# Two-layer SSD and dilated-attention trunk on one core: another load order and more warm-up matmuls at the start, another PSUM tile for the first group's scores, regrouped centring matmuls at the end

## The chip, the cores and the metric

The kernel runs on one core of a Trainium2 chip. The metric is the device time of one execution in microseconds, as the median of several runs. Engines are named as in the profile: PE is TensorE's matmuls, PEld its weight loads, DVE VectorE, ACT ScalarE, POOL GpSimd, SP the engine that issues most transfers (SPq is its queue).

## The reference

A batch of one, 256 tokens of width 2048, two layers. Layer 0 is a Mamba-2 SSD mixer with 64 heads in 8 groups; layer 1 is dilated sliding-window attention with keys and values made once from layer 0's output. Both layers are scaled, shifted and gated from a conditioning row `c` (adaLN), and end in a layer norm.

```python
def reference(x, c, ada_w, ada_b, ln_g, ln_b, a_in_w, a_conv_w, ..., kv_w, b_in_w, b_out_w):
    for layer in range(DEPTH):                      # 2
        shift, scale, gate = _adaln(c, ada_w[layer], ada_b[layer])   # split(silu(c) @ w + b, 3)
        h = x * (1.0 + scale) + shift
        if layer < N_A_LAYERS:
            y = _ssd_mixer(h, ...)     # proj, causal conv + silu, chunked scan, silu gate, RMS norm, out_w
        else:
            y = _dilated_mixer(h, k_sh, v_sh, b_in_w[i], b_out_w[i])
        x = _layer_norm(DEEPNORM_ALPHA * x + (1.0 + gate) * y, ln_g[layer], ln_b[layer])
        if layer == N_A_LAYERS - 1:
            k_sh, v_sh = _shared_kv(x, kv_w)
    return x
# in the scan, one chunk of 256 tokens:
cb = jnp.einsum("blgn,bsgn->blsg", cc, bc)          # the scores of a group
y_diag = jnp.einsum("blsgk,bsgkp->blgkp", cb[..., None] * decay, xc)
```

## The kernel before, in words

All weights stream from HBM in pieces of 128 x 1024 float32 (512 KB, tile `raw`, six buffers). A piece is split into a high part (`whi`, ACT, L100) and a low part (`wlo`, DVE, L102), four buffers each, and each product is the sum of high by high, high by low and low by high (L151 to L153, L190 and L193, L232 to L234). The activations (`actT`) are split in the same way. A program written in Python issues the instructions; a scheduler then sets the order on each engine from the dependences and a cost model, and `issue_after` pins an instruction behind another. Each engine works through its own order strictly in sequence. Transfers use eight completion semaphores in turn, so each issue on SP waits for the transfer eight places before it.

**Start.** Layer 0's scale and shift are not matmuls: the conditioning row is broadcast to 128 partitions by 16 matmuls against identity columns (L473, into `cps`), ACT applies SiLU (L476, `cb_`), and DVE takes 32 products of 128 x 2048 with a summed output (`araw`, L501, L503, L317), one per 128 columns of scale or shift, each from a transfer of 1 MB. Their order is scale 0, shift 0, scale 1, shift 1 and so on. Then DVE adds the bias (L322, `mod`), and ACT makes `htmp` (L522) and its high part (L524). `warm(n, at)` issues n matmuls of ones (L460) so that PE is not idle before the real work: a group ahead of the broadcast and one behind it. The first three weight pieces come in halves: `begin_piece(i)` loads the first half (L557), `end_piece(i)` the second (L560). `plain` multiplies the first halves, unsplit, with `htmp` (L572); then the first products with split weights start at L151.

**SSD stage.** For each group, `stage1` computes the scores of B and C in three blocks (L742, L743) into a PSUM tile, evicts them to `cb` (L745 with the causal mask, L746), builds the decays `seg` on ACT from `cumT` (L756, L758), multiplies them with `cb` (L759), and transposes x (L767). `stage2` multiplies `seg` and `xd` (L800, `py`). PSUM there is `mm` (four `acc` tiles) and two pools of two tiles, `aux` and `aux2`; `aux2` holds only `py`. Ahead of group 0, DVE computes softplus and the cumulative decays (L709 to L721), PE sums them (L723, L724), and SP writes them out (L734) and reads them back broadcast (`cbc`, L751). All of this is interleaved with the projection products of the next groups.

**End.** The last layer norm, for the second half of the rows, is made on PE as a sum of two matmuls per chunk of 512 columns: `plus` adds the weighted chunk by an identity (L1318), `centre` subtracts mean times weight by a diagonal (L1322); chunk 3 is done on DVE (`between`, L1326). `root` computes the reciprocal standard deviation; DVE scales the chunks (L1341) and SP stores each (L1269).

Of the kernel before, what the change touches and what calls it, by code (L numbers as in the profile page):

```python
# [9 lines left out]
F32 = mybir.dt.float32  # L10
F32R = mybir.dt.float32r
I32 = mybir.dt.int32
AF = mybir.ActivationFunctionType
ALU = mybir.AluOpType
# [4 lines left out]
P = 128  # L19
# [30 lines left out]
def trunk(ctx, tc, xT, x, c, par, cst, bias, lnrow, ada, wdt, win, wxs, wout, wk, wv, wbin, wbout, out):  # L50
# [9 lines left out]
    aux = None  # L60
# [295 lines left out]
    with ExitStack() as cA:  # L356
# [15 lines left out]
        with ExitStack() as cS:  # L372
# [78 lines left out]
            with ExitStack() as c0:  # L451
# [11 lines left out]
                at = mm.tile([P, 2, L], F32, name="acc")  # L463
                last = warm(6, at)
                crow2 = pe.tile([48, P + KT], F32R, name="crow", bufs=1)
                V.tensor_copy(crow2, crow)
                V.tensor_tensor(crow2[32:, :P], crow[32:, :P], crow2[32:, :P].bitcast(F32), op=ALU.subtract)
                with tc.tile_pool(name="ec", bufs=4, space=PSUM) as ec:
                    for n in range(4):
# [6 lines left out]
                        S.activation(cb_[:, 512 * n:512 * n + 512], cps, AF.Silu)  # L476
                    last = warm(14, at, last)
                ex = c0.enter_context(tc.tile_pool(name="ex", bufs=4, space=PSUM))
# [110 lines left out]
                fetch_x(0)  # L589
                fetch()  # L590
                fetch()
                begin_piece(0)
                begin_piece(1)
# [142 lines left out]
            def stage1(g):  # L736

                pcb = aux.tile([P, 512], F32, name="aux")[:, :384].rearrange("p (a n) -> p a n", a=3)  # L740
                bm, cm_ = bc[g][:, 0, :], bc[g][:, 1, :]
# [528 lines left out]

    diag = pc2.tile([P, 512], F32, name="sc0", bufs=1)[:, :P]
    eps, sd = sm.tile([P, 1], F32, name="nm"), sm.tile([P, 1], F32, name="den")
# [51 lines left out]
    def between(mv):  # L1324
        V.tensor_scalar(diag, ident, mv[:, 0:1], -1.0, op0=ALU.mult, op1=ALU.mult)
        return V.scalar_tensor_tensor(u[1][:, chunk[3]], u[1][:, chunk[3]], mv[:, 0:1], lnt[:, 0, chunk[3]],  # L1326
                                      op0=ALU.subtract, op1=ALU.mult)

    plus(1, plus(0, end))
    _, r1, step = root(1, between)  # L1330
    centre(0)
    plus(2, centre(1))
    for h in range(2):
        centre(2, slice(256 * h, 256 * h + 256))
    for c in chunk:
        scaled(0, c)
        nc.gpsimd.dma_start(rows(out, 0)[:, c], u[0][:, c], accum_op=ALU.add)
    for n, h0, h1 in ((0, 0, 512), (1, 0, 512), (3, 0, 512), (2, 0, 256), (2, 256, 512)):
        c = slice(512 * n + h0, 512 * n + h1)
        with tc.issue_after(step.ins):  # L1340
            step = V.scalar_tensor_tensor(u[1][:, c], cen[n][:, h0:h1] if n < 3 else u[1][:, c], r1, lnt[:, 1, c],  # L1341
                                          op0=ALU.mult, op1=ALU.add)
        store(1, c)
# [95 lines left out]
```

## Time and profile before

| | |
|---|---|
| median of 3 runs | 1226.51 us (1226.43 to 1226.7) |
| profiled execution | 1226.18 us, span 1224.4 us |
| PE, PEld, DVE, ACT busy | 99%, 85%, 83%, 58% of the span |
| transfers | 331.45 MB read, 3.23 MB written, mean 273 GB/s over the span |
| chain that ended last | PE 83%, DMA 9%, DVE 5%, ACT 2% |

A row of the timeline gives start, duration, engine, line, operation, tiles and count; in brackets stands how long the engine had been idle and what ended that. A float32 matmul leaves two records of PE. Ends of matmuls are modelled, so successive ones overlap. In the table of stretches the columns are the stretch, its length, PE's busy time with the count of matmuls, the granted clock, the busy share of the transfer engines and GB/s; where no engine is chosen, PE, PEld, DVE, ACT and POOL stand in this order ahead of the clock. A row of waits gives the sum, the number and the longest wait.

### The profile page before, as it was taken

What the parts mean: (1) busy time and instruction counts of PE and PEld (TensorE: products, weight loads), DVE (VectorE), ACT (ScalarE), POOL (GpSimd) and SP (SyncE); (2) the same over time, 40 slices, a digit from 0 to 9 for tenths busy, and PEclk for the clock granted to TensorE, in tenths of its full rate; (3) what the DMA queues carried; (4) which work ended last, traced back from release to release, by engine and by line L of the source; (5) the groups of instructions that cost most, each with busy time, mean ns of one, the idle gap of its engine ahead of it and who ended that gap; (6) DMA issues with size and microseconds to landing.
All of it is one profiled execution on the core that took longest, in us unless ns stands there. A gap on an engine that the chain in (4) does not pass through costs nothing.

```text
span 1224.4 us, 19063 instructions
## 1 busy us (share of the span) xinstructions
PE 1210.7 (99%) x7244; PEld 1039.0 (85%) x7244; DVE 1018.5 (83%) x1448; ACT 707.2 (58%) x1058; POOL 3.9 (0%) x8
## 2 busy tenths in 40 slices
PE   8899999999999999999999999999999999999998
PEld 7889988898888888878888888888888888888886
DVE  6999996999988989899778588888987875756886
ACT  4555477878597789754445455444435844444751
POOL 0000000000000000000000000000000000000001
PEclk9999999999999999999999999999999999999999
DMA  9999986687666556689998669989997885365673
GB/s 370 422 421 422 421 279 246 228 300 246 222 205 206 172 173 208 214 322 328 390 308 295 222 194 345 344 343 385 369 389 279 285 262 174 111 193 161 194 258 69
DMA packets 81372, 335.94 MB, mean 274 GB/s; under 512 B 9200, under 2 KB 9984, under 8 KB 68480
## 3 DMA queue, kind: packets, MB, share of 16 engines
q1 hardware_dynamic: 80496, 333.59, 75.3%
q0 software_dynamic: 576, 1.05, 0.6%
q8 instruction: 57, 0.93, 0.3%
q14 instruction: 35, 0.29, 0.1%
q10 hardware_dynamic: 208, 0.08, 0.0%
HBM read 331.45 MB, written 3.23 MB: 273 GB/s over the span
## 4 chain that ended last, share of the span: by engine, by line
PE 83%; DMA 9%; DVE 5%; ACT 2%; issue 1%; SPq 0%; ACTq 0%; DVEq 0%
PE acc L190 24%; PE acc L224 24%; PE acc L193 12%; DMA raw<-in_win 5%; PE acc L233 4%; PE acc L234 4%; PE acc L232 4%; DMA araw<-in_ada 3%; DVE araw L317 2%; DVE wlo L102 1%; PE acc L153 1%; PE acc L151 1%; PE py L800 1%; PE acc L152 1%; ACT whi L100 1%
## 5 line engine op out<-in xcount | busy, mean ns | idle before, releaser
L100 ACT ACTIVATE whi<-raw 128x1024 fp32r<-128x1024 f32 x389 | 408.9, 1057 | 355.0 <-PE acc L190 106.5
L102 DVE TENSOR_TENSOR wlo<-raw,whi 128x1024 fp32r<-128x1024 f32 x389 | 469.3, 1220 | 136.2 <-ACT whi L100 126.0
L190 PE MATMUL acc<-actT,whi 128*128 128x512 f32 x1280 | 401.1, 394 | 0.0
L193 PEld LDWEIGHTS acc<-actT,wlo 128*128 128x128 f32 x1280 | 239.5, 188 | 52.5 <-DVE wlo L102 0.3
L193 PE MATMUL acc<-actT,wlo 128*128 128x256 f32 x1280 | 254.7, 280 | 0.0
L317 DVE SCALAR_TENSOR_TENSOR araw<-araw,cb__72 128x2048 f32<-128x2048 f32 x95 | 216.9, 2284 | 2.7 <-DMA araw<-in_ada 2.3
L190 PEld LDWEIGHTS acc<-actT,whi 128*128 128x128 f32 x1280 | 194.7, 188 | 0.8
L224 PE MATMUL acc<-whi,actT 128*128 128x512 f32 x560 | 144.4, 392 | 0.5 <-ACT whi L100 0.5
L224 PEld LDWEIGHTS acc<-whi,actT 128*128 128x128 f32 x560 | 104.1, 188 | 22.1 <-ACT whi L100 0.9
L233 PE MATMUL acc<-wlo,actT 128*128 128x512 f32 x272 | 107.0, 393 | 2.6 <-DVE wlo L102 2.6
L151 PE MATMUL acc<-actT,whi 128*128 128x256 f32 x372 | 103.2, 281 | 1.2 <-ACT s L657 1.0
L232 PE MATMUL acc<-whi,actT 128*128 128x512 f32 x272 | 104.3, 394 | 0.0
L224 PE MATMUL acc<-wlo,actT 128*128 128x512 f32 x384 | 103.5, 391 | 0.0
L153 PE MATMUL acc<-actT,wlo 128*128 128x256 f32 x372 | 101.7, 282 | 1.6 <-DVE wlo L102 1.4
L152 PE MATMUL acc<-actT,whi 128*128 128x256 f32 x372 | 102.8, 279 | 0.0
L234 PE MATMUL acc<-whi,actT 128*128 128x512 f32 x256 | 100.2, 391 | 0.0
L224 PEld LDWEIGHTS acc<-wlo,actT 128*128 128x128 f32 x384 | 71.6, 188 | 14.5
L151 PEld LDWEIGHTS acc<-actT,whi 128*128 128x128 f32 x372 | 69.6, 188 | 2.7 <-ACT s L657 1.4
L153 PEld LDWEIGHTS acc<-actT,wlo 128*128 128x128 f32 x372 | 68.8, 188 | 2.9 <-DVE wlo L102 2.7
L152 PEld LDWEIGHTS acc<-actT,whi 128*128 128x128 f32 x372 | 70.5, 189 | 0.5 <-issue 0.2
L233 PEld LDWEIGHTS acc<-wlo,actT 128*128 128x128 f32 x272 | 51.1, 188 | 14.7 <-DVE wlo L102 4.5
L232 PEld LDWEIGHTS acc<-whi,actT 128*128 128x128 f32 x272 | 50.7, 188 | 9.9
(321 smaller groups left out, 1296.3 us busy)
## 6 DMA issues: line engine op xcount, KB each, us to landing
araw<-in_ada SPq DMA_DIRECT2D x96, 1024.0 KB, 7.4
raw<-in_win SPq DMA_DIRECT2D x109, 512.0 KB, 6.2
raw<-in_wout SPq DMA_DIRECT2D x64, 512.0 KB, 5.8
raw<-in_wbin SPq DMA_DIRECT2D x64, 512.0 KB, 4.2
raw<-in_wxs SPq DMA_DIRECT2D x48, 512.0 KB, 4.5
raw<-in_wv SPq DMA_DIRECT2D x48, 512.0 KB, 6.8
raw<-in_wk SPq DMA_DIRECT2D x48, 512.0 KB, 8.1
cbc<-cumd SPq DMA_DIRECT2D x16, 512.0 KB, 5.6
```

What stands on the lines that cost most here:

```text
L100: copied.append(S.activation(hi, raw, AF.Copy))
L102: latest.append(V.tensor_tensor(lo, raw, hi.bitcast(F32), op=ALU.subtract))
L151: T.matmul(o, hi[:, k, c_], ahi[:, kt, :], start=first, stop=False, skip_group_check=True)
L152: T.matmul(o, hi[:, k, c_], alo[:, kt, :], start=False, stop=False, skip_group_check=True)
L153: T.matmul(o, lo[:, k, c_], ahi[:, kt, :], start=False, stop=kt == k1 - 1, skip_group_check=True)
L190: T.matmul(ps[n], hi[:, k, n * P:n * P + P], both(kt), start=kt == 0, stop=False, skip_group_check=True)
L193: T.matmul(ps[n][:, 0, :], lo[:, k, n * P:n * P + P], high(kt), start=False, stop=kt == KT - 1, skip_group_check=True)
L224: T.matmul(ps[b], a_(kt)[:, b * P:b * P + P], w_[:, k, :], start=a_ is ahi and w_ is hi and kt == k0, stop=w_ is lo and kt == k1 - 1)
L232: T.matmul(o, h_, hi[:, k, :], start=kt == k0, stop=False, skip_group_check=part)
L233: T.matmul(o, h_, lo[:, k, :], start=False, stop=False, skip_group_check=part)
L234: end = T.matmul(o, l_, hi[:, k, :], start=False, stop=kt == k1 - 1, skip_group_check=part)
L317: return V.scalar_tensor_tensor(raw, raw, 1.0, cb_, op0=ALU.mult, op1=ALU.mult, accum_out=mod[layer][:, ct, j:j + 1])
```

## The change

Four edits.

1. Seven more warm-up matmuls: 11 instead of 6 ahead of the broadcast, 16 instead of 14 behind it.
2. The first half of weight piece 0 is loaded ahead of the second adaLN scale.
3. The scores of SSD group 0 go to a tile of `aux2` (named `py`) instead of one of `aux`.
4. At the end all three `plus` products precede the `centre` products; the diagonal is made by ACT from a negated identity (`minus`, made earlier by DVE) instead of by DVE; chunk 3 is scaled first.

```diff
                 at = mm.tile([P, 2, L], F32, name="acc")
-                last = warm(6, at)
+                last = warm(11, at)
...
-                    last = warm(14, at, last)
+                    last = warm(16, at, last)
...
                 fetch()
                 fetch_x(0)
                 fetch()
+                begin_piece(0)
                 fetch()
-                begin_piece(0)
                 begin_piece(1)
...
-                pcb = aux.tile([P, 512], F32, name="aux")[:, :384].rearrange("p (a n) -> p a n", a=3)
+                pcb = aux2.tile([P, 512], F32, name="py") if g == 0 else aux.tile([P, 512], F32, name="aux")
+                pcb = pcb[:, :384].rearrange("p (a n) -> p a n", a=3)
...
-    diag = pc2.tile([P, 512], F32, name="sc0", bufs=1)[:, :P]
+    pair = pc2.tile([P, 512], F32, name="sc0", bufs=1)
+    diag, minus = pair[:, :P], pair[:, P:2 * P]
+    V.tensor_scalar(minus, ident, -1.0, None, op0=ALU.mult)
...
     def between(mv):
-        V.tensor_scalar(diag, ident, mv[:, 0:1], -1.0, op0=ALU.mult, op1=ALU.mult)
+        S.activation(diag, minus, AF.Copy, scale=mv[:, 0:1])
...
-    plus(1, plus(0, end))
+    plus(2, plus(1, plus(0, end)))
     _, r1, step = root(1, between)
     centre(0)
-    plus(2, centre(1))
+    centre(1)
...
-    for n, h0, h1 in ((0, 0, 512), (1, 0, 512), (3, 0, 512), (2, 0, 256), (2, 256, 512)):
+    for n, h0, h1 in ((3, 0, 512), (0, 0, 512), (1, 0, 512), (2, 0, 256), (2, 256, 512)):
```

Lines behind the third edit move down by one, those behind the fourth by three: L742 becomes L743, L800 becomes L801, L1341 becomes L1344.

What this does to the order is seen at three places. First SP's transfers at the start, before (`araw` are adaLN pieces, `raw` weight pieces, here halves; DMAHW0 to 7 are the eight semaphores):

```order
L310 DMA araw_180<-in_ada 128x2048
L490 DMA xt_182<-in_xT 128x512
L310 DMA araw_184<-in_ada 128x2048
L310 DMA araw_186<-in_ada 128x2048
L557 DMA raw_188<-in_win 128x512
L557 DMA raw_190<-in_win 128x512
L310 DMA araw_192<-in_ada 128x2048 [waits DMAHW0_49]
```

and after:

```order
L310 DMA araw_187<-in_ada 128x2048
L490 DMA xt_189<-in_xT 128x512
L310 DMA araw_191<-in_ada 128x2048
L557 DMA raw_193<-in_win 128x512
L310 DMA araw_195<-in_ada 128x2048
L557 DMA raw_197<-in_win 128x512
L310 DMA araw_199<-in_ada 128x2048 [waits DMAHW0_49]
```

The first half piece and the second scale have changed places; the rest of the queue stands as it was.

Second, PE in the last product of z for group 0 (`acc`, with the high and low weights `whi` and `wlo`), before:

```order
L232 MATMUL acc_1965<-whi_1987,actT_84 128x512 [waits Activation_49]
L232 MATMUL acc_1966<-whi_1987,actT_84 128x512
L233 MATMUL acc_1965<-wlo_1988,actT_84 128x512 [waits DVE_49]
L234 MATMUL acc_1965<-whi_1987,actT_84 128x512
L233 MATMUL acc_1966<-wlo_1988,actT_84 128x512
```

and after (`bcm` are B and C of group 0):

```order
L232 MATMUL acc_1972<-whi_1994,actT_84 128x512 [waits Activation_49]
L232 MATMUL acc_1973<-whi_1994,actT_84 128x512
L743 MATMUL py_2283<-bcm_1878 128x2x128 [waits DVE_49]
L744 MATMUL py_2283<-bcm_1878 128x128
L233 MATMUL acc_1972<-wlo_1995,actT_84 128x512 [waits DVE_49]
L234 MATMUL acc_1972<-whi_1994,actT_84 128x512
```

The scores stand about 195 matmuls earlier than before, in front of a product that waits for DVE. On DVE the end of the decay chain (`araw` is its scratch, `dtT` and `cumT` its results) reads before:

```order
L717 SCALAR_TENSOR_TENSOR araw<-araw 128x128 [waits DVE_49]
L718 SCALAR_TENSOR_TENSOR araw<-araw 128x128 [waits DVE_49]
L719 SCALAR_TENSOR_TENSOR dtT<-vv,araw 128x128 [waits DVE_49]
L721 SCALAR_TENSOR_TENSOR araw<-dtT,araw 128x128 [waits DVE_49]
L102 TENSOR_TENSOR wlo<-raw,whi 128x1024 [waits DMAHW0_49,Activation_49]
```

and after:

```order
L717 SCALAR_TENSOR_TENSOR araw<-araw 128x128 [waits DVE_49]
L746 TENSOR_TENSOR cb<-py,cc 128x256
L718 SCALAR_TENSOR_TENSOR araw<-araw 128x128 [waits DVE_49]
L747 COPY cb<-py 128x128
L719 SCALAR_TENSOR_TENSOR dtT<-vv,araw 128x128 [waits DVE_49]
L102 TENSOR_TENSOR wlo<-raw,whi 128x1024 [waits DMAHW0_49,Activation_49]
L721 SCALAR_TENSOR_TENSOR araw<-dtT,araw 128x128 [waits DVE_49]
```

The two evictions of the scores and one split of a weight piece have moved ahead of L721, whose result PE's L723 waits for. From here to about 500 us the order of the SSD stage differs on all engines.

Third, PE at the end (`u` is the residual, `cc` the constants with the identity, `sc` the diagonal), before:

```order
L1318 MATMUL aux_11762<-u1_5575,cc_76 128x512
L1318 MATMUL aux_11763<-u1_5575,cc_76 128x512 [waits DVE_49]
L1322 MATMUL aux_11762<-actT_11404,sc0_11603 128x512 [waits DMAHW2_49,DVE_49]
L1322 MATMUL aux_11763<-actT_11404,sc0_11603 128x512
L1318 MATMUL po_11764<-u1_5575,cc_76 128x512
L1322 MATMUL po_11764<-actT_11404,sc0_11603 128x256 x2
```

and after:

```order
L1321 MATMUL aux_11770<-u1_5582,cc_76 128x512
L1321 MATMUL aux_11771<-u1_5582,cc_76 128x512 [waits DVE_49]
L1321 MATMUL po_11772<-u1_5582,cc_76 128x512 [waits DVE_49]
L1325 MATMUL aux_11770<-actT_11411,sc0_11610 128x512 [waits DMAHW2_49,Activation_49]
L1325 MATMUL aux_11771<-actT_11411,sc0_11610 128x512
L1325 MATMUL po_11772<-actT_11411,sc0_11610 128x256 x2
```

The third identity product now comes ahead of the first diagonal one, which waits for ACT instead of DVE.

## The prediction, made before the changed kernel was run

> **What bounds the kernel now.** I read the page first, then the matmul engine's busy time in stretches of 20 us, then the timeline at the three places that the change touches.
>
> ```profile
> PE 1210.7 (99%) x7244; PEld 1039.0 (85%) x7244; DVE 1018.5 (83%) x1448; ACT 707.2 (58%) x1058; POOL 3.9 (0%) x8
> ```
> ```profile
> 0.00:20.00 20.00, 16.75 (x80) 1.00 0.91 342
> 20.00:40.00 20.00, 18.71 (x134) 1.00 1.02 422
> 40.00:60.00 20.00, 18.00 (x125) 1.00 1.02 420
> ...
> 180.00:200.00 20.00, 19.55 (x94) 1.00 0.60 208
> ...
> 240.00:260.00 20.00, 20.00 (x162) 1.00 0.91 334
> ...
> 460.00:480.00 20.00, 20.00 (x120) 1.00 0.78 260
> ```
>
> TensorE is busy for 1210.7 of 1224.4 us, so everything that idle time could ever give back is 13.7 us, and the change removes no useful matmul. The idle time lies in the first 60 us (3.25 + 1.29 + 2.00 of it), in the stretch with one hole near 187 us (0.45), and later; the twelve stretches from 240 to 480 us have 0.01 together. In the first 60 us the fourth column, the transfer engines' busy share, is already 1.02: there the matmuls run out because weights have not arrived. Besides idle time, the first 14.87 us hold only warm-up and broadcast matmuls, and the last 9 us a tail of dependent work. So there are three terms: the start, the hole at 187 us, the tail.
>
> **The start.** Warm-up matmuls (two records each), broadcast of the conditioning row, first adaLN products, first product with weights:
>
> ```profile
> 1.09 2.93 PE L460 MATMUL acc<-ones 128*128 128x128 f32 x12 [1.09 <-DVE ones L455]
> 5.90 3.67 PE L473 MATMUL cps<-crow 48*128 48x128 f32 x16 [1.88 <-DVE crow L467]
> 8.53 1.23 DVE L501 SCALAR_TENSOR_TENSOR araw<-araw,cb__72 128x1024 f32<-128x1024 f32 x1 [2.69 <-ACT cb__72 L476]
> 9.50 5.08 PE L460 MATMUL acc<-ones 128*128 128x128 f32 x28
> 11.58 2.28 DVE L317 SCALAR_TENSOR_TENSOR araw<-araw,cb__72 128x2048 f32<-128x2048 f32 x1
> 14.21 0.60 ACT L522 ACTIVATE htmp<-xt,mod 128x256 f32<-128x256 f32 x1 [4.01 <-DVE mod L322]
> 14.87 5.45 PE L572 MATMUL acc<-htmp,raw 128*128 128x256 f32 x24 [0.28 <-ACT htmp L522]
> 16.87 2.29 DVE L317 SCALAR_TENSOR_TENSOR araw<-araw,cb__72 128x2048 f32<-128x2048 f32 x1
> 20.51 0.74 PE L151 MATMUL acc<-actT,whi 128*128 128x256 f32 x4 [0.19 <-ACT actT L524]
> ...
> 27.31 2.29 DVE L317 SCALAR_TENSOR_TENSOR araw<-araw,cb__72 128x2048 f32<-128x2048 f32 x1 [0.55 <-DMA araw<-in_ada]
> ```
> ```profile
> 13.13 0.33 SPq L90 DMA_DIRECT2D raw<-in_win  x1
> 13.81 0.33 SPq L310 DMA_DIRECT2D araw<-in_ada  x1
> ...
> 16.91 0.33 SPq L310 DMA_DIRECT2D araw<-in_ada  x1
> ```
>
> The transfer queue keeps eight transfers in flight, and each issue waits for the one eight places before it. So the issue times tell landings: the second adaLN scale had landed at 13.13, the first half piece at 13.81, the second shift at 16.91. After the change the half piece goes first: it lands one megabyte earlier, at 400 GB/s (the rate of these windows is below) 2.6 us, so near 11.2; the scale takes the place at 13.8. Nothing behind the two moves, since the bytes ahead of them are the same; SP issues the next weight piece about 1.9 us earlier, into a queue that is full anyway.
>
> Five more warm-up matmuls are ten records of 2.93/12 = 0.244 us: they fill the idle time from 4.02 to 5.90 and end near 6.3 at that spacing, 5.95 at the 0.22 of back-to-back starts. At worst the broadcast starts 0.4 us late, at best it runs at the fast pace, seen in these counts (16 matmuls in the second stretch against 11):
>
> ```profile
> 10.00:12.00 2.00, 2.00 (x11) 2.00 (x10) 1.73 (x4) 0.21 (x1) 0.00 (x0) 1.00 0.98 408
> 12.00:14.00 2.00, 2.00 (x16) 2.00 (x15) 1.98 (x3) 0.00 (x0) 0.00 (x0) 1.00 1.04 399
> ```
>
> The clock column says 1.00 in both, though the pace doubles within the second; I go by the pace. The Trainium skill, "TensorE: Matmul & The Clock Gate", Part 1, says the array starts at half clock and is released after a free-running window of about 3.4 us of sustained work, and falls back after an idle one as long. By that rule the old 2.93 us could not open it before the broadcast and about 4.9 us may; the trace agrees as far as 5.90 to about 13 us stayed slow.
>
> At the fast pace the broadcast takes about 1.9 instead of 3.67 us, and the row is ready some 1.1 us earlier (four ACT pieces of 0.60 then set the pace). The first adaLN product starts near 7.9 instead of 8.53; the first shift's, now bound by its own landing (13.13 less the scale's 2.6, so 10.5), a microsecond earlier than 11.58; the first weight product near 13.95 instead of 14.87, its half piece being there. But the next step needs the second shift, whose product at 16.87 starts as it lands (16.91 is the issue that waited for the same transfer). From there to 20.51 every time is as before; the 24 matmuls only end a microsecond earlier and wait. At 27.31 DVE again waits for an adaLN transfer. So 0.92 us saved at 14.87 turns into 0.9 us more wait at 20.5. Two more matmuls in the second warm-up are 4 records, 0.4 (fast) to 0.9 us (slow), under the same cover. The term: 0, between -0.9 (all of it carries through) and +0.2 (slow pace: 28 records ended at 14.58, 32 end near 15.0, and the 24 then end 0.15 late).
>
> **The hole at 187 us.** Scores of SSD group 0, formerly at 215.90:
>
> ```profile
> 186.38 1.22 DVE L102 TENSOR_TENSOR wlo<-raw,whi 128x1024 fp32r<-128x1024 f32 x1
> ...
> 193.83 0.29 DVE L721 SCALAR_TENSOR_TENSOR araw<-dtT,araw 128x128 f32<-128x128 f32 x1
> ...
> 217.84 0.41 DVE L745 TENSOR_TENSOR cb<-aux,cc 128x256 f32<-128x256 f32 x1
> ...
> 220.92 0.28 DVE L746 COPY cb<-aux 128x128 f32<-128x128 f32 x1
> ```
> ```profile
> 186.58 0.61 PE L232 MATMUL acc<-whi,actT 128*128 128x512 f32 x2
> 187.65 0.50 PE L233 MATMUL acc<-wlo,actT 128*128 128x512 f32 x1 [0.45 <-DVE wlo L102]
> ...
> 194.38 0.38 PE L723 MATMUL aux<-araw,cc 128*128 128x128 f32 x2
> ```
> ```profile
> 215.90 0.60 PE L742 MATMUL aux<-bcm 128*128 128x256 f32 x2
> ...
> 216.55 0.60 PE L767 MATMUL aux<-cc,xs 128*128 128x128 f32 x4
> ...
> 226.49 1.15 PE L800 MATMUL py<-xd,seg 128*64 128x64 f32 x30
> ```
>
> With their own PSUM tile the scores stand, in the new order, between the two L232 and the L233 that waits for the low half. They cost 216.55 - 215.90 = 0.65 us. The second L232 starts 0.23 after 186.58, so the next matmul could start at 187.04 and the hole is 0.61 wide (0.45 as the busy time is modelled). What they wait for on DVE stands there ahead of the split at 186.38, so it is over. The L233 starts about 0.05 late, and 0.65 go at 215.9: -0.60. Only the modelled 0.45 usable would make it -0.45.
>
> What pays: DVE now does the two score evictions (0.41 + 0.28) ahead of the decay chain, and a 1.22 split too, so L721 ends at 194.12 + 0.41 + 0.28 + 1.22 = 196.0 instead of 194.12, or near 195.5, since DVE steps that do not depend on each other overlap by some 0.08 (L1326 below starts at 1216.57, before L1325 ends at 1216.65) and the dependent ones no longer stand back to back. I take 195.5. L723 waits for it, but stands six matmuls later in the new order: 35 instead of 29 after L233, at 6.73/29 = 0.232 us, thus at 195.8. So no wait; at the pessimistic end 0.2. SP's copy of the cumulative decays then goes out about 2 us later, behind one more weight load, and ACT's exponentials with it:
>
> ```profile
> 213.47 1.04 ACT L758 ACTIVATE seg<-seg 128x1024 f32<-128x1024 f32 x1
> ```
>
> They ended at 214.51, and are needed, after a 1.22 DVE product, by L800 at 226.49: over 10 us of room, 2 to 2.5 used. The DVE work before L800 shrinks by the 0.69 that was done early. With next to no idle time from 240 to 480 us the matmul engine sets the pace there, so the advance should last. Term: -0.6, from -0.65 to -0.2.
>
> **The tail.** Chain of waits, then DVE, and the price of an ACT operation on 128x128:
>
> ```profile
> 1215.08 1.72 PE aux L1318 x4
> 1216.80 1.89 PE aux L1322 x4
> ```
> ```profile
> 1216.36 0.29 DVE L1325 TENSOR_SCALAR sc<-cc,e1mv 128x128 f32<-128x128 f32 x1
> 1216.57 0.75 DVE L1326 SCALAR_TENSOR_TENSOR u<-u,e1mv,actT 128x512 f32<-128x512 f32 x1
> ...
> 1220.45 0.88 DVE L1341 SCALAR_TENSOR_TENSOR u<-po,e1y,actT 128x256 f32<-128x256 f32 x2 [0.31 <-PE po L1322]
> ```
> ```profile
> 177.07 0.31 ACT L710 ACTIVATE araw<-araw 128x128 f32<-128x128 f32 x1
> ```
>
> All three L1318 pairs now precede the L1322 pairs. The L1322 group took 1.89 against 1.72 for the same amount of L1318: 0.17 us is its wait for the diagonal. With a third pair (0.86) ahead, L1322 can start at 1217.5. The diagonal moves to ACT behind the square root, 0.31 from about 1216.75, ready at 1217.1. So the matmuls run through, 0.17 earlier at the end. DVE gains 0.21 at 1216.36, and takes the fourth chunk, which needs no matmul, first; it then follows PE. Its last two pieces waited until 1220.45 for both halves of the last group, and will again: -0.17. Were each half awaited alone, it would be -0.4; with DVE late behind the reordered chunks, 0. The negated identity on DVE (0.29, as L1325) lies long before, in slack. The last store follows the last piece as before.
>
> **Sum.** 0 - 0.6 - 0.17 = about -0.8 us on the profiled execution, which took 1226.18 (span 1224.4 and 1.8 around it), 0.3 below the median of 1226.51. Against the median: 1225.7.
>
> **The rivals.**
> *The start carries through.* The landings are not as strict as I read them, and the 0.92 us stay gained: 1226.51 - 0.77 - 0.92 = 1224.8. For it: PE does idle at 20.51 for an ACT result. Against: DVE's start at 16.87 coincides with a landing, and it waits for another at 27.31. Chance 0.11. If instead the clock fell back in the longer gap before 13.95, the 24 matmuls would take twice 5.45 us and end 4.4 us later, of which the 3.3 us of idle time up to 60 us hide most: about 1226.8; 0.03.
>
> *The fill is given back.* The scheduler's whole order from 187 to 500 us changes, and a new wait of half a microsecond at L723 or at a later group takes the 0.6 back: 1226.3, up to 1226.8. For it: DVE is 83% busy on average, so a bad order costs at once. Against: the nearest waits come out with room. Chance 0.20.
>
> *Slower.* SP works in order, and the decay copies now stand behind a load that waits for a free buffer. In this trace such a wait reaches 11.9 us:
>
> ```profile
> SPq L90 <- DVE wlo L102: 48.3, 21, 11.9
> ```
>
> If it fell there, on top of the 2 us, L800 would start some 4 us late (13.9 against 10 of room): 1225.7 + 4 = 1229.7. It decides once the copies are more than 10 us late. Against: the load in front frees its buffer with the very split that DVE does just before the copy's source. Chance 0.03.
>
> **Chances and range.** My forecast has 0.61; 0.02 stay for what I have not seen. The likeliest case alone spans 1225.3 to 1226.2. The start's carrying through at the low end and the give-back at the high end, with the 0.13 by which runs differ (1226.43 to 1226.70), give 1224.6 to 1226.9. What measurement can tell from no change is 0.2%, 2.45 us: all but the slower rival and unseen cases lie within it. Faster 0.04, same 0.92, slower 0.04.
>
> **What would show it.** Right: first weight product near 14 us but L151 still at 20.5; no hole at 187 us, the transposes near 216.0 with the scores gone; L1322 following L1318 without a gap, and an end about 0.8 us earlier. Wrong: L151 earlier than 20.3 with later stages shifted alike; a new wait at L723 or L801 (the former L800); or an idle PE where the order was rewritten.

## The result, and the profile after

The changed kernel took 1234.13 us in the median of five runs (1232.41 to 1234.55), the kernel before 1226.51: the ratio is 1.0056, with an interval of 1.0041 to 1.0070. So it is slower, by some 7 us, where 1225.7 was forecast and 1226.9 was the upper end. The profiled execution took 1232.41 us with a span of 1230.6, 6.2 more than before.

The engines on the page of the changed kernel:

```profile
PE 1214.0 (99%) x7258; PEld 1041.5 (85%) x7258; DVE 1018.6 (83%) x1448; ACT 704.0 (57%) x1057; POOL 3.9 (0%) x8
```

TensorE is busy 3.3 us longer, with matmuls of the same work plus 14 warm-up records, and idle 2.9 us longer. Busy time beyond what the records account for is a slower pace. The stretches say where (busy time of PE, PEld, DVE, ACT, POOL, then clock, transfer share, GB/s). Before:

```profile
200.00:220.00 20.00, 20.00 (x159) 19.41 (x158) 11.41 (x16) 18.11 (x33) 0.00 (x0) 1.00 0.86 309
220.00:240.00 20.00, 19.91 (x150) 16.06 (x149) 20.00 (x31) 16.65 (x32) 0.00 (x0) 1.00 0.53 173
```

and after:

```profile
200.00:220.00 20.00, 20.00 (x166) 19.44 (x165) 8.31 (x10) 15.88 (x28) 0.00 (x0) 1.00 0.87 289
220.00:240.00 20.00, 17.09 (x116) 13.09 (x115) 18.33 (x30) 16.75 (x32) 0.00 (x0) 0.83 0.39 121
280.00:300.00 20.00, 19.38 (x159) 16.05 (x158) 20.00 (x32) 12.15 (x25) 0.00 (x0) 1.00 0.43 153
```

From 220 to 240 us TensorE loses 2.91 us to idle time, and its clock was granted at 0.50 for a third of it (0.83 is the mean; the edges are shown in the last section). VectorE, which is full in this stretch before, does 3.1 us less in the 20 us ahead of it. TensorE's timeline after, from 222 us (the row of L801 in the prediction is its counterpart):

```profile
222.65 0.61 PE L232 MATMUL acc<-whi,actT 128*128 128x512 f32 x2
225.68 1.98 PE L801 MATMUL py<-xd,seg 128*64 128x64 f32 x32 [2.41 <-DVE xd L770]
228.15 2.05 PE L790 MATMUL aux<-xo,cb 128*128 128x512 f32 x2 [0.49 <-DVE xo L778]
230.12 1.98 PE L801 MATMUL py<-xd,seg 128*64 128x64 f32 x32
232.03 0.55 PE L233 MATMUL acc<-wlo,actT 128*128 128x512 f32 x1
```

Two waits for VectorE, 2.41 + 0.49 = 2.90. Then 32 records of L801 take 1.98 where the kernel before had 30 in 1.15, and so on until 232: three groups at half pace, 6.0 us of work that is 3.5 at full pace (1.15, 1.12 and 1.26 before), another 2.5. Together 5.4 us are lost within ten microseconds.

The rest of the account compares the two kernels at the same instruction. At the hole near 187 us the changed kernel is 1.0 us late already, but a second profile of the unchanged kernel is so too (below), so that this need not be the change's. At the L232 of 222.65, the 25th z product (L232 to L234) behind the run of L151 to L153, it is 0.55 us ahead (223.20 before): the filled hole has returned 0.65; the 144 products of L151 to L153 just before start every 0.113 us instead of every 0.118, another 0.6, for a reason that was not found; and a short wait ahead of the transposes at 221.35 is gone, 0.25. The ten microseconds then make it 5.0 late. Another 1.5 go by 500 us: waits of 0.62 at 297.76 us (in the stretch from 280) and 0.17 at 321.09 can be seen, the rest is spread over small pieces. The tail returns 0.2. So the order of the SSD stage gains some 1.5 us up to 222 us, loses 5.5 in the next ten, and by 500 us loses again about what it had gained.

What made VectorE late is told by three engines' rows. SP's queue before, and after (`cumd` the copy out, `cbc` the copy back):

```profile
196.62 0.51 SPq L734 DMA_DIRECT2D cumd<-araw  x1
199.89 1.82 SPq L751 DMA_DIRECT2D cbc<-cumd  x2
```
```profile
199.44 1.14 SPq L734 DMA_DIRECT2D cumd<-araw  x1
202.57 0.33 SPq L90 DMA_DIRECT2D raw<-in_win  x1
204.02 0.81 SPq L752 DMA_DIRECT2D cbc<-cumd  x2
```

ACT's first read of the decays before, and after:

```profile
203.56 1.56 ACT L756 ACTIVATE seg<-cbc,cumT 128x128 f32<-128x128 f32 x5
```
```profile
209.61 1.57 ACT L757 ACTIVATE seg<-cbc,cumT 128x128 f32<-128x128 f32 x5 [2.99 <-DMA cbc<-cumd]
```

VectorE after:

```profile
212.16 1.23 DVE L102 TENSOR_TENSOR wlo<-raw,whi 128x1024 fp32r<-128x1024 f32 x1 [4.29 <-ACT whi L100]
215.71 1.23 DVE L760 TENSOR_TENSOR seg<-seg,cb 128x1024 f32<-128x1024 f32 x1 [2.32 <-ACT seg L759]
218.71 1.23 DVE L102 TENSOR_TENSOR wlo<-raw,whi 128x1024 fp32r<-128x1024 f32 x1 [1.77 <-ACT whi L100]
```

The copy out is 2.8 us late, the copy back 4.1, with a load of weights now in between, and the first read 6.05. The place of the load does not hold the copy back: SP has issued it by 202.90 and then still waits 1.1 us for the copy out to land. ACT, which waited for nothing here before, stands 2.99 us; the weight splits of L100 and the exponentials of L759 behind it in its order stand too, and VectorE waits for these: 4.29, 2.32 and 1.77. In all VectorE is idle for 11.7 us from 200 to 220, where it was idle for 8.6 before. The chain of waits from 198 us to the first late product runs through the same places (start, duration, what):

```profile
199.44 4.56 DMA cumd<-araw
...
204.02 5.57 DMA cbc<-cumd
...
217.73 0.96 ACT whi L100
...
218.71 1.23 DVE wlo L102
219.94 1.20 DVE s L443 x2
221.13 1.13 DVE seg L760
222.27 2.76 DVE cacc L390 x7
225.03 0.60 DVE xd L770
```

Two transfers take 10 us, ACT follows, and then VectorE works without a break until `xd`, for which L801 waits.

### The profile page after: what moved, and what is told of

Same layout as the page of the kernel before. It is cut to its first block, busy times and chain, and to the rows that moved or that the text cites. A ratio compares the mean times of both kernels' runs of the same rounds, so it can differ in the third digit from the quotient of the medians.

```text
span 1230.6 us, 19092 instructions
## 1 busy us (share of the span) xinstructions
PE 1214.0 (99%) x7258; PEld 1041.5 (85%) x7258; DVE 1018.6 (83%) x1448; ACT 704.0 (57%) x1057; POOL 3.9 (0%) x8
## 4 chain that ended last, share of the span: by engine, by line
PE 81%; DMA 7%; DVE 7%; ACT 3%; issue 2%; DVEq 0%; ACTq 0%; SPq 0%
PE acc L224 25%; PE acc L190 23%; PE acc L193 12%; DMA raw<-in_win 5%; PE acc L233 4%; PE acc L234 4%; PE acc L232 4%; DVE araw L317 2%; DVE wlo L102 2%; PE py L801 1%; ACT whi L100 1%; DMA araw<-in_ada 1%; PE acc L153 1%; PE acc L151 1%; PE acc L152 1%
## 5 line engine op out<-in xcount | busy, mean ns | idle before, releaser
L100 ACT ACTIVATE whi<-raw 128x1024 fp32r<-128x1024 f32 x389 | 408.6, 1057 | 355.5 <-PE acc L190 108.9
L233 PE MATMUL acc<-wlo,actT 128*128 128x512 f32 x272 | 107.2, 394 | 1.9 <-DVE wlo L102 1.9
L151 PE MATMUL acc<-actT,whi 128*128 128x256 f32 x372 | 103.3, 282 | 2.0 <-ACT s L657 1.1
L232 PE MATMUL acc<-whi,actT 128*128 128x512 f32 x272 | 104.4, 394 | 0.0
L153 PE MATMUL acc<-actT,wlo 128*128 128x256 f32 x372 | 102.2, 282 | 1.5 <-DVE wlo L102 1.3
L234 PE MATMUL acc<-whi,actT 128*128 128x512 f32 x256 | 100.2, 391 | 0.0
L151 PEld LDWEIGHTS acc<-actT,whi 128*128 128x128 f32 x372 | 69.7, 188 | 3.5 <-ACT s L657 1.5
L153 PEld LDWEIGHTS acc<-actT,wlo 128*128 128x128 f32 x372 | 68.9, 188 | 2.8 <-DVE wlo L102 2.8
L233 PEld LDWEIGHTS acc<-wlo,actT 128*128 128x128 f32 x272 | 51.2, 188 | 14.2 <-DVE wlo L102 3.8
L232 PEld LDWEIGHTS acc<-whi,actT 128*128 128x128 f32 x272 | 50.7, 188 | 10.3 <-ACT s L657 0.5
```

The source lines that it names most:

```text
L100: copied.append(S.activation(hi, raw, AF.Copy))
L151: T.matmul(o, hi[:, k, c_], ahi[:, kt, :], start=first, stop=False, skip_group_check=True)
L153: T.matmul(o, lo[:, k, c_], ahi[:, kt, :], start=False, stop=kt == k1 - 1, skip_group_check=True)
L232: T.matmul(o, h_, hi[:, k, :], start=kt == k0, stop=False, skip_group_check=part)
L233: T.matmul(o, h_, lo[:, k, :], start=False, stop=False, skip_group_check=part)
L234: end = T.matmul(o, l_, hi[:, k, :], start=False, stop=kt == k1 - 1, skip_group_check=part)
```

## The experiments

Each ratio is against the kernel before, measured beside it in five rounds (one round for the rerun of it), with its 95% interval. The expectations name the theories by letters. Theory A: VectorE is late, because the early evictions delay the decay copies. Theory B, for the first four runs alone: the start's edits make the later work late. Rival C: the new order on TensorE puts the group's products L801 and L790 too early (after some 26 matmuls of z instead of some 38, about 3 us), so that they stop the queue for results that would have been in time at their old place. Rival D, for `early_decays` alone: the evictions, or the moved order, cost by themselves.

**One part of the change at a time.** `no_scores` is the change without its third edit, and the other three are the kernel before with one edit (the two of the start count as one).

```diff
-                pcb = aux2.tile([P, 512], F32, name="py") if g == 0 else aux.tile([P, 512], F32, name="aux")
-                pcb = pcb[:, :384].rearrange("p (a n) -> p a n", a=3)
+                pcb = aux.tile([P, 512], F32, name="aux")[:, :384].rearrange("p (a n) -> p a n", a=3)
```

> The changed kernel with the scores of group 0 back in the old PSUM pool: start and end changed alone. Theory A (the scores' new place makes the loss, by a late decay chain and a clock drop near 225 us): the idle time at 223 us and the half-pace stretch behind it are gone, and what is left is the start (0.2 to 0.6 us late at 60 us) and the end (-0.2): 1226.3 to 1227.2 us. Theory B (the start's shift of the transfers by up to 0.7 us makes the later work late, and the scores only add to it): at least half of the loss stays, 1229.5 us or more, with idle time of PE in 200 to 240 us.

> The kernel before with the other PSUM pool for the scores of group 0 alone. Theory A: the whole loss but the start's share: PE idles about 2 us near 223 us, then runs at half pace for about 6 us; 1231.5 to 1234 us. Theory B: without the start's shift the decays come in time, and it ends below 1229 us. The prediction on record would have 1225.9.

> The kernel before with the first two edits alone (more warm-up, the first half weight piece ahead of the second scale). Theory A: the transfers of 20 to 60 us run 0.2 to 0.7 us later than before and PE with them, partly given back later: 1226.5 to 1227.3 us. Theory B: 1228 us or more, with new idle time of PE behind 200 us. The prediction on record had it at 1226.5 with 1225.6 if the start carries through.

> The kernel before with the regrouped end alone. Every theory: the time up to 1215 us as before, the last piece 0.17 us earlier: 1226.2 to 1226.4 us, which the measurement may not tell from no change.

Measured: without the scores' edit 1.0005 (0.9996 to 1.0014), the scores alone 1.0041 (1.0028 to 1.0054), the start 1.0010 (1.0001 to 1.0019), the end 1.0002 (0.9993 to 1.0011). The loss is the third edit's, 5 us of it, and the start adds about one; theory B falls. TensorE with the scores alone:

```profile
224.76 1.15 PE L801 MATMUL py<-xd,seg 128*64 128x64 f32 x32 [1.47 <-DVE xd L770]
227.23 1.10 PE L790 MATMUL aux<-xo,cb 128*128 128x512 f32 x2 [1.32 <-DVE xo L778]
```

The two waits add up to almost as much as in the full change (1.47 + 1.32 = 2.79 against 2.90), but the groups run at full pace, 1.15 and 1.10. So the pace is no condition of a loss here, though it makes the change's larger: this profile loses 3.1 us in the ten microseconds where the change loses 5.5. It has waits of 0.25 behind the groups and of 0.44 at 282.99 that the change has not. One of 1.22 at 987.95 us belongs to no edit of this place, since `no_scores` has one of 1.28 there and the change none.

**Late VectorE or early products.** `evict_late` holds the two evictions back behind the copy out's source; `products_late` holds the group's products behind the z product of the next group; `both_late` does both; `changed_again` is the change.

```diff
-            V.tensor_copy(cumr, pr)
+            cum_out = V.tensor_copy(cumr, pr)
...
+                with tc.issue_after(cum_out.ins) if g == 0 else ExitStack():
+                    V.tensor_tensor(cb[:, 0:2, :], pcb[:, 0:2, :], tri[:, None, :].to_broadcast([P, 2, P]), op=ALU.mult)
+                    V.tensor_copy(cb[:, 2, :], pcb[:, 2, :])
```
```diff
+                with tc.issue_after(z_end[-1].ins) if g == 0 else ExitStack():
+                    T.matmul(po, cb[:, 2, :], xo, start=True, stop=True)
...
-                behind = z_end[-1] if g in (4, 7) else None
+                behind = z_end[-1] if g in (0, 4, 7) else None
```

> The changed kernel as it is, on this chip beside the next three. If its loss is a property of the order, it is 5 to 8 us slower than before, with idle time of PE ahead of the first L801 near 223 to 226 us. If PE stands idle for about 2.4 us there, the products behind it run at half pace (1.98 us for 32) until about 232 us, and it is at the upper end; if for 1.5 us, at full pace (1.15), and it is at the lower end.

> The changed kernel with the two evictions of the early scores held behind the copy of the cumulative decays on VectorE; the scores themselves stay in the hole at 187 us. The transfers of the decays then stand in SP's queue as in the kernel before, while PE's products of group 0 (L802 here) stay some 40 matmuls earlier than before. Theory A (the decay chain, made late by the evictions and by a weight load ahead of the decays' copy back, makes the loss): no idle time over 0.5 us at 223 us, 1226 to 1228 us. Rival C (the earlier place of the products in PE's order makes it, whatever the decays do): PE idles 1.5 us or more ahead of them, 1230 us or more. The prediction on record would have had 1225.9 for both this kernel and the changed one.

> The changed kernel with the first group's L790 and L801 held behind the whole z product of group 1, so about 9 us later in PE's order; the decay chain stays as late as in the changed kernel. Theory A in its strict form (lateness alone decides): other work that hangs on the decays waits and most of the loss stays, 1230 us or more. Rival C: the loss is gone, 1226 to 1228 us. Between them, theory A with cover (idle time is the lateness less the work that stands ahead of the products): gone as well, since 9 us of cover is more than the 2.4 us missed.

> Both holds together: evictions behind the decays' copy, products of group 0 behind the z product of group 1. Any theory: no idle time at 223 us. If the scores in the hole at 187 us are worth what was forecast, and the wait of L767 for the score eviction (0.7 to 1.5 us in the kernels with the old PSUM pool on this chip) goes too, it ends at 1225.5 to 1227, ahead of the kernel before by 0.5 us or more; if later groups give it back, 1227 to 1228.5.

Measured: the change 1.0046 (1.0033 to 1.0058); evictions late 1.0011 (1.0002 to 1.0019); products late 1.0097 (1.0084 to 1.0110); both 1.0040 (1.0026 to 1.0054). Holding the evictions back takes away all but what the start alone costs; holding the products back doubles the loss. With the evictions late, SP, ACT and TensorE read:

```profile
201.47 0.81 SPq L753 DMA_DIRECT2D cbc<-cumd  x2
```
```profile
205.71 1.58 ACT L758 ACTIVATE seg<-cbc,cumT 128x128 f32<-128x128 f32 x5 [1.24 <-DMA cbc<-cumd]
```
```profile
225.01 1.10 PE L791 MATMUL aux<-xo,cb 128*128 128x512 f32 x2 [1.34 <-DVE xo L779]
```

ACT's wait is 1.24 instead of 2.99, and TensorE's 1.34 instead of 2.90, at full pace; theory A had expected 0.5 at most. What is left of ACT's wait and the early place of the products were not separated there. With the products late TensorE reads, and with both late:

```profile
230.43 0.80 PE L233 MATMUL acc<-wlo,actT 128*128 128x512 f32 x1 [7.34 <-DVE wlo L102]
```
```profile
226.56 0.50 PE L233 MATMUL acc<-wlo,actT 128*128 128x512 f32 x1 [3.17 <-DVE wlo L102]
```

What TensorE reaches instead of the held products is a weight product whose low half VectorE has not split, since the split stands behind the same backlog, and the wait there is longer. `both_late` was expected to have no idle time here and has 3.17 us of it, though ACT's wait for the decays is down to 1.64, so that holding the products back costs by itself. The hold moved them by some 9 us, further than to their old place, which no run tested alone. But the change's own trace shows what would stand there: the next z product needs the low half that VectorE splits from 229.30 to 230.5 us, later than `xd` at 225.6. So the products' place alone does not make the loss: VectorE is late, and whatever TensorE does next waits for it. Rival C falls as the whole cause.

**The unchanged kernel, decays that need not come back, and two attempts at a better kernel.** `before_again` is the kernel before. `other_decays` and `early_decays` let the first group read its decays from the adaLN weights (so their values are others); the first is held behind the copy out, the second is not.

```diff
+                    src = ada if g == 0 else cumd
+                    with tc.issue_after(cum_sent.ins) if g == 0 else ExitStack():
-                    nc.sync.dma_start(cbc, bass.AP(tensor=cumd.tensor, offset=cumd.offset + h0 * L,
+                        nc.sync.dma_start(cbc, bass.AP(tensor=src.tensor, offset=src.offset + h0 * L,
```

`xo_late` is `evict_late` with L791, whose wait remained, held behind the z product. `best_try` is that with the start of the kernel before.

> The kernel before as it is, profiled on the chip of these runs. If ScalarE's first read of the decays waits 0.3 to 0.6 us for their transfer here (as with the end alone changed) and PE idles 0.5 to 0.8 us ahead of L767 near 222 us, the start's two edits cost at most the rest of what the start alone showed, 0.6 us; if neither waits (as in the profile given first), the start's edits cost about 1.2.

> The changed kernel where the first group's decays are read from the adaLN weights in memory, right behind the copy out, so that no transfer waits for the decays' landing; its output is not the reference's for that. Evictions, split and copy out stay as late as in the changed kernel. Theory A (the wait for the decays' round trip through memory, passed on by ScalarE and VectorE): ScalarE doesn't wait at its first read, VectorE is busy for 10.5 to 12 us of 200 to 220 us instead of 8.4, PE loses less than 1.5 us in 220 to 240 us, 1226.5 to 1229 us. If it stays above 1231, the early evictions cost by themselves, not through the decays.

> Evictions behind the decays' copy as before, and only L791 (the product that PE waited 1.34 us for) held behind the z product of group 1, while the products with seg and xd, which were ready there, stay early. If that wait was the whole loss left at this place: no idle time over 0.4 us in 220 to 240 us, 1227 to 1228.2 us. If VectorE's splits are late there anyway (as with both products held back, 3.17 us), an idle time of 1 us or more stays, 1228.5 us or more.

> The same with the start of the kernel before: scores in the hole, evictions behind the decays' copy, L791 held back, new end. If the start's edits cost 0.6 to 1.2 us, the scores gain 0.5 and the end 0.17: 1226 to 1227.3, at or ahead of the kernel before. If the place near 223 us is as tight as before: the same as before within 0.1%.

> The changed kernel, early evictions and all, where the first group's decays are read from the adaLN weights in memory and without a place behind the copy out, so that both transfers go out some 8 weight pieces earlier, long before ScalarE wants them; its output is not the reference's for that. Theory A (the decays' transfers, waited for by ScalarE, then VectorE, then TensorE, make the loss): ScalarE's first read of them has no wait, VectorE is busy for 10.5 us or more of 200 to 220 us, TensorE for 19 or more of 220 to 240 us, 1226 to 1228 us. Rival D (the evictions and the split on VectorE ahead of the chain cost by themselves, or the moved order does): VectorE's load there stays below 9.5 us and it is 1230 us or more.

Measured: the kernel before again, 1.0000 (0.9988 to 1.0013). In its profile the L233 of the hole stands at 188.77, 1.1 us later than in the first profile and as late as in the change; so that microsecond differs between runs. `other_decays` 1.0027 (1.0015 to 1.0040), `xo_late` 1.0011 (1.0002 to 1.0019), `best_try` 1.0006 (0.9997 to 1.0015), `early_decays` 1.0012 (1.0003 to 1.0021).

`other_decays` didn't take the wait away: its transfers were issued at 200.57, and ACT's first read still waited 2.79 us for them, to 207.15. So it says nothing about a kernel without the wait, only that a copy back that needs nothing from the copy out is late as well when it is issued there. `early_decays`, whose transfers went out at 176.47, did:

```profile
200.00:220.00 20.00, 20.00 (x162) 19.54 (x161) 13.04 (x16) 17.71 (x29) 0.00 (x0) 1.00 0.80 287
220.00:240.00 20.00, 20.00 (x157) 16.74 (x156) 20.00 (x30) 14.16 (x24) 0.00 (x0) 1.00 0.59 207
```
```profile
293.63 0.51 PE L193 MATMUL acc<-actT,wlo 128*128 128x256 f32 x2 [1.56 <-DVE wlo L102]
```

ACT waits for nothing at its first read (which also stands earlier in its order, at 198.94), VectorE is busy 13.04 us before 220, and TensorE has no idle time from 220 to 240, with the early evictions and the early products both in place. That the late return of the decays makes the loss there is thus shown, and rival D falls for this place. But the kernel gains nothing over the one before (its 1228.6 us are above the 1228 that theory A allowed): its waits come at 279.72 (0.52), 281.17 (0.38) and 293.63 (1.56), 2.46 in all in a stretch that had none. The fill of the hole is spent later in this order too. And `xo_late` moved its wait, as `products_late` had: 2.08 at an L233 in place of 1.34 at L791. `best_try` came within 0.1% of the kernel before, as was expected if this place stayed as tight as it was.

**The start, its two edits apart, and the harmless edits together.** `warm_only` is the kernel before with the warm-up matmuls, `load_only` with the first half piece ahead, `load_end` with that and the end's edit.

```diff
-                last = warm(6, at)
+                last = warm(11, at)
...
-                    last = warm(14, at, last)
+                    last = warm(16, at, last)
```

> The kernel before with the seven more warm-up matmuls alone. The prediction on record has 0 for them, and the start's two edits together measured +0.1%. If the warm-up makes that (its faster broadcast moves ScalarE's and VectorE's first work): 1228.2 to 1229 us; if the load order does: as before, 1227.5.

> The kernel before with the first half weight piece ahead of the second adaLN scale alone. If the load order makes the start's +0.1%: 1228.2 to 1229 us; if the warm-up does: 1227.5. If each shows less than 0.05%, the start's cost is not told from no change.

> The kernel before with the load order and the regrouped end, without the extra warm-up and without the scores' new place: the two edits that cost nothing alone. Sum of the parts: load order -0.04% (interval -0.13 to +0.04), end -0.17 us: 1226.5 to 1227.3 us where before is 1227.2 to 1227.6, the same or ahead by up to 0.1%. If it is 1228 or more, the round trip of the decays (3.0 to 3.3 us from the copy out to the copy back in the profiles without the extra warm-up and with late evictions, 3.9 to 5.0 in the others) moves for another reason than the warm-up.

Measured: 1.0012 (1.0003 to 1.0020), 0.9996 (0.9987 to 1.0004), 0.9996 (0.9987 to 1.0005). The load's place does nothing that can be measured, the warm-up matmuls cost about 1.4 us (0.4 to 2.5 by the interval). No version here beats the kernel before. In `warm_only`'s timeline the start reads

```profile
15.50 7.13 PE L572 MATMUL acc<-htmp,raw 128*128 128x256 f32 x24 [3.78 <-ACT htmp L522]
```

which is the forecast's rival of a clock that falls back in the longer gap, though not in the change itself, where the half piece came first and the gap was 1.71.

**One number for all of them.** Seven of these kernels, those without the scores' edit, have the order of before on VectorE and TensorE at this place. One of them, with the end's edit:

```profile
200.00:220.00 20.00, 20.00 (x162) 19.56 (x161) 10.83 (x13) 18.56 (x32) 0.00 (x0) 1.00 0.81 292
220.00:240.00 20.00, 19.32 (x143) 15.32 (x142) 20.00 (x32) 15.77 (x31) 0.00 (x0) 1.00 0.52 179
```
| kernel | ACT's first wait for the decays | VectorE busy, 200 to 220 | less than before | TensorE busy, 220 to 240 | less than before |
|---|---|---|---|---|---|
| before, `load_only` | 0 | 11.41 | 0 | 19.91 | 0 |
| `before_again` | 0 | 11.17 | 0.24 | 19.66 | 0.25 |
| `end_only` | 0.48 | 10.83 | 0.58 | 19.32 | 0.59 |
| `warm_only` | 0.91 | 10.40 | 1.01 | 18.90 | 1.01 |
| `start_only` | 1.10 | 10.22 | 1.19 | 18.71 | 1.20 |
| `load_end` | 0.25 | 10.16 | 1.25 | 18.66 | 1.25 |
| `no_scores` | 1.27 | 10.04 | 1.37 | 18.54 | 1.37 |

Each microsecond that VectorE does not work before 220 us is a microsecond of TensorE's idle time behind it. A row is one execution and need not belong to the edit beside it: `end_only` and `load_end`, whose edits lie far from this place and whose ratios are 1.0002 and 0.9996, lose 0.59 and 1.25 here, so that the wait for the decays also varies from run to run in the old order. The change itself, in its own order, has 3.10 less of the one and 2.82 of the other, half pace apart. (`load_end` waits a second time for the decays, which the column of its first wait doesn't count.)

## Why the prediction was wrong, by its own steps

**The start** was right in what was forecast: the first weight product came near 14 us and the next step at the old time.

```profile
13.92 5.75 PE L572 MATMUL acc<-htmp,raw 128*128 128x256 f32 x24 [1.71 <-ACT htmp L522]
20.65 0.74 PE L151 MATMUL acc<-actT,whi 128*128 128x256 f32 x4 [0.98 <-ACT actT L524]
```

13.95 was forecast, and 20.51 became 20.65: the advance went into the wait of 0.98. The term of 0 holds for the load. For the warm-up matmuls it was mis-sized: bounded at +0.2, it measured about +1.4. In the profile of `warm_only` the cost does not show behind the start (against the first profile of the kernel before it is 0.5 us late at 60 us, and `before_again` 0.7) but at 223 us, where the transposes wait 1.10 us for VectorE. Yet `load_end`, without these matmuls, waits 1.34 there and is not slower in the median; so where the cost arises, and how, stays open.

**The hole** was filled as forecast, and the nearest waits were right to a tenth of a microsecond:

```profile
187.58 0.62 PE L232 MATMUL acc<-whi,actT 128*128 128x512 f32 x2
188.03 0.59 PE L743 MATMUL py<-bcm 128*128 128x256 f32 x2
188.46 0.38 PE L744 MATMUL py<-bcm 128*128 128x128 f32 x2
188.64 0.50 PE L233 MATMUL acc<-wlo,actT 128*128 128x512 f32 x1
```
```profile
196.24 0.28 DVE L721 SCALAR_TENSOR_TENSOR araw<-dtT,araw 128x128 f32<-128x128 f32 x1
...
198.95 0.41 DVE L733 COPY araw<-aux 64x256 f32<-64x256 f32 x1
```

L233 follows the scores without a wait. This stage runs 0.99 us late (188.64 against 187.65); without that, L721 ends at 195.53 (195.5 forecast), and the copy out goes 2.82 - 0.99 = 1.8 us late ("about 2"). The load in front of the copy back was forecast too.

**The step that failed** is the next one: "needed, after a 1.22 DVE product, by L800 at 226.49: over 10 us of room, 2 to 2.5 used". Both halves were off. The delay was 5 us (6.05 - 0.99) by the time ACT read the decays, since the copy out is answered later (4.6 instead of 3.3 us from issue to issue) and the copy back needed 5.57 (in the kernel before ACT read it without a wait 3.67 us after its issue). And the room was nil. It was counted from the exponentials to the one product that uses them, as if nothing else hung on ACT and VectorE. But ACT's wait holds the weight splits behind it, these hold VectorE, and VectorE is full afterwards: the row of before from 220 to 240 says 20.00 of 20.00. An engine that is full for the next 20 us, and on which TensorE waits in that stretch, can give back no lost microsecond; the table above shows it one for one. The profile of before had this row, and the prediction read TensorE's column of it alone. The other 2.5 us of the ten, the half pace behind the wait, had no term at this place; the prediction weighed a fall of the clock only for the start.

**The range** was also too narrow for the noise. Its 0.13 us came from three runs; in the later rounds the kernel before ran between 1225.7 and 1231.8, with medians of 1227.2 to 1227.7.

**The rivals.** The slower one, with 0.03, named the right copies and the right direction for another reason. Its load in front of the copy back did wait for a buffer, 1.9 us, but within the time that the copy out took to land, so that this wait cost nothing. It put the point from which lateness decides at "more than 10 us late", by the same room; 2.8 us at the copy out were enough. Its 1229.7 would also have been too low. "The fill is given back" came true beside it: 0.62 us at 297.76, and 2.46 us in `early_decays`, in orders whose cost the nearest waits could not tell.

**The tail** was right: -0.17 was forecast. The profile shows the identity products ahead and the diagonal ones without a gap:

```profile
1223.04 1.02 PE L1321 MATMUL po<-u,cc 128*128 128x512 f32 x2
1223.90 1.88 PE L1325 MATMUL aux<-actT,sc 128*128 128x512 f32 x4
1225.62 1.03 PE L1325 MATMUL po<-actT,sc 128*128 128x256 f32 x4
1226.68 0.88 DVE L1344 SCALAR_TENSOR_TENSOR u<-po,e1y,actT 128x256 f32<-128x256 f32 x2
```

The last pieces come 6.23 us later than before, where the same stage began 6.41 later (1221.53 against 1215.12 at the first DVE row of it): -0.18. The timing of the end's edit alone, 1.0002 with an interval of 0.18%, is too coarse to show it.

## What to carry to other kernels

The room of a late result is not the time until its own reader starts: follow what stands behind each engine that waits for it, in order, and ask whether any engine on the way is full in the stretch that follows. If one is, and the bounding engine reads from it, count no room. Where a step is moved ahead of the source of a round trip through memory, put the round trip's whole delay into the sum, a slower answer and a slower copy back included, and not the step's own duration.

## What the hardware showed that was not expected

**The pace after a gap.** After 2.41 us of idle time in the change (2.35 in its second profile) the granted clock fell to 0.50, and half pace lasted to 232, some 6 us. In `xo_late` 2.08 us were enough, with half pace until 230.2, and 3.78 us in `warm_only` slowed the start. Yet after 3.17 us in `both_late` the clock stayed at 1.00, and after 1.47 and 1.32 with the scores alone as well. So the length of the gap does not decide alone.

Its place does. In every trace here the clock changes only at steps of 3.41 us: in the change it rises at 6.89 us, falls at 225.34, 64 steps later, and rises again at 232.17, two more. These are the steps at the gap, first in the change and then in `both_late`, counted on from its clock's first rise at 6.73 (TensorE's busy time, with modelled ends, clock, transfers):

```profile
221.93:225.34 3.41, 1.33 (x6) 1.00 0.24 95
225.34:228.75 3.41, 2.58 (x33) 0.50 0.00 0
228.75:232.17 3.42, 3.42 (x35) 0.50 0.21 26
```
```profile
221.77:225.18 3.41, 1.62 (x8) 1.00 0.08 31
225.18:228.60 3.42, 2.04 (x9) 1.00 0.29 63
```

The change has 2.08 us of idle time in one step, and the clock falls at its end. The longer gap of `both_late` lies across an edge, 1.79 us on one side and 1.38 on the other, and the clock stays. Counted so in all eighteen traces from 12 us to 1220, the clock fell behind the steps with 1.90 us (`xo_late`), 1.96 (`load_only`, at 31.78) and more, and stayed behind those with 1.82 or less; behind 1220 us, one step of 1.95 in the tail of `xo_late` had no fall. From 12 us on the clock rose again behind the first step that was busy throughout, or all but 0.18 us. Among the warm-up and broadcast matmuls of the first 12 us it fell behind less idle time, 0.55 to 1.35. The Trainium skill, "TensorE: Matmul & The Clock Gate", Part 1, tells of a window of about 3.4 us that runs freely, and of a fall after an idle one. The steps agree with that window; that it must be idle throughout does not, since some 1.9 us of 3.41 were enough here.

**The answer of a small copy.** From the issue of the copy out to that of the copy back it took 3.0 to 3.3 us in six profiles without the extra warm-up matmuls and with late or no early evictions, 3.9 to 5.0 in the six with the warm-up matmuls and no early evictions, and 4.0 to 4.6 in the four with early evictions (one of them without the warm-up matmuls, the scores alone, with 4.18). If the warm-up matmuls at 1 us are behind this, how they change an answer at 200 us was not found.
